# Projection weights by halves of their rows: four raw halves, rings of three split halves in place of two whole blocks

## The chip, the cores and the metric

The kernel runs on one core of one Trainium2 chip. The metric is the device time of one execution in microseconds (us); lower is better. Durations and waits come from one profiled execution, whose engines are named PE (matmul), PEld (PE's weight loads), DVE, ACT, POOL and SP. SP does no arithmetic here: it issues most DMAs, one after the other in a fixed order.

## The reference, cut to what matters

A two-layer encoder trunk over two sequences of 512 and 2048 tokens, T = 2560 tokens in all, width 1024:

```python
p = _rmsnorm(x, norm_w) @ w_in                 # layer 0: 1024 -> 4224 columns
y_a = _rwkv7(r, k, v, w_lat, a_lat, ...)       # a recurrence over tokens, both directions
y_b = _dilated_attention(_rope(q_b), _rope(k_b), v_b)
x = x + concat(y_a * silu(gate_a), y_b * silu(gate_b)) @ w_out
p = _rmsnorm(x, norm_w) @ w_in                 # layer 1: 1024 -> 3088 columns
y = _gla(q, k, v, gate_lat, ...) * silu(gate)  # chunked gated linear attention, both directions
x = x + y @ w_out
```

The change touches the two products with `w_in`, the input projections. All is float32.

## The kernel before, in words

**The projections.** Tokens are taken in five tiles of 512, output columns in blocks of 128: 33 blocks of layer 0 and 25 of layer 1 (one of them 16 columns wide). For a token tile `xprep` (lines 228 to 253) loads and normalises x, transposes it to eight tiles of 128 features by 512 tokens, and splits each into a high part `xh` and a low part `xl` of a reduced float type. `dense` (line 273) then goes through the blocks. The weights of a block are eight slices of 128 rows (k = 0 to 7). Each weight is split in the same way into `wh` and `wl`, and the product is the sum of three: wh·xh + wh·xl + wl·xh. So a block is 24 matmuls of 128x128 by 128x512 on line 287, summed into one bank `pd` of PSUM (two such banks take turns). In most blocks the 16 matmuls with `wh` come first and the 8 with `wl` after them; in the first and last block of a tile's pass the three of each k stand together. There are 5 · 33 + 5 · 25 = 290 blocks in the program; the first 165 of them, of layer 0, are called blocks 0 to 164 here, in the order in which they run.

**How a block's weights come.** `wfetch` (line 255) issues on SP two DMAs of 256 KB (line 258), rows k = 0 to 3 into tile `w0`, rows 4 to 7 into `w1`. Each of the two has one buffer. `wsplit` (line 262) makes `wh` and `wl` for all eight k: of the first half DVE rounds `w` to `wh` (line 266) and subtracts to get `wl` (line 267); of the second half ACT rounds and POOL subtracts. The tiles `wh` and `wl` hold a whole block and have two buffers each. In 4-byte words of a partition that is 2 · 512 raw and 4 · 1024 split, 20 KB.

A raw buffer is free again when its subtraction is done; a buffer of `wh` or `wl` when the last matmul of the block that reads it is done.

**What follows a block.** `even_sink` and `odd_sink` empty the bank: a copy to `st` on ACT (line 307) for the RWKV columns, two products with the rotary tables on DVE (line 317), or a tanh on ACT and a product on DVE (line 341) for the gates.

**What lies beside.** Layer 0: while tile n is projected, `prep` (line 400) makes the recurrence's factors of tile n - 1, with work on all engines and stores of 1 MB (`d_f`, line 480), and `inverts` (line 546) runs long sequences of small DVE operations. Then the recurrence of layer 0 runs beside attention, then the output projection of layer 0 (line 1022), then the projections of layer 1 partly beside the GLA scans, and at the end the output projection of layer 1.

**What sets the order.** Generators are woven by ratio (`mix`) into one program order; a scheduler then lays out every engine's instructions by a simulated time line. The result is one fixed list for each engine (and for each DMA issuer); on the chip each works through its list strictly in order, and an instruction that waits holds back all behind it. `order` rows below are pieces of these lists.

Of the kernel before, what the change touches and what calls it, by code (L numbers as in the profile page):

```python
# [11 lines left out]
F32 = mybir.dt.float32  # L12
F32R = mybir.dt.float32r
# [3 lines left out]
OP = mybir.AluOpType  # L17
# [100 lines left out]
class Trunk:  # L118
# [133 lines left out]
            yield 430  # L252
        xT[:] = tiles

    def wfetch(self, src, m):
        ws = [self.wpool.tile([128, 4, 128], F32, name=f"w{h}", bufs=1) for h in range(2)]
        for h, w in enumerate(ws):
            self.nc.sync.dma_start(w[:, :, :m], src[:, 4 * h:4 * h + 4])
        return ws

    def wsplit(self, ws, m):
        nc = self.nc
        wh, wl = (self.wpool.tile([128, 8, 128], F32R, name=n, bufs=2) for n in ("wh", "wl"))
        for h, (w, e) in enumerate(zip(ws, (nc.vector, nc.gpsimd))):
            k = slice(4 * h, 4 * h + 4)
            (nc.vector.tensor_copy, nc.scalar.copy)[h](wh[:, k, :m], w[:, :, :m])  # L266
            e.tensor_tensor(wl[:, k, :m], w[:, :, :m], wh[:, k, :m].bitcast(F32), op=OP.subtract)  # L267
        return wh, wl

    def dense(self, parts, xT=None):  # L270

        nc = self.nc
        flat = [(p, n, *job) for p, (_, jobs) in enumerate(parts) for n, job in enumerate(jobs)]
        cur = self.wsplit(self.wfetch(*flat[0][2:4]), flat[0][3])
        xT = [] if xT is None else xT
        for i, (p, n, _, m, sink) in enumerate(flat):
            if n == 0 and parts[p][0]:
                yield from parts[p][0](xT)
            wh, wl = cur
            if i + 1 < len(flat):  # L280
                cur = self.wsplit(self.wfetch(*flat[i + 1][2:4]), flat[i + 1][3])
            ps = self.pd.tile([128, 512], F32, name="pd")
            three = [((wh, k, hi), (wh, k, lo), (wl, k, hi)) for k, (hi, lo) in enumerate(xT)]
            byk = n == 0 or n == len(parts[p][1]) - 1
            three = [e for t in three for e in t[:3 if byk else 2]] + [t[2] for t in three if not byk]
            for j, (a, k, x) in enumerate(three):
                nc.tensor.matmul(ps[:m], a[:, k, :m], x, start=j == 0, stop=j == 23)  # L287
                if j % 6 == 5:
                    yield 1280
            sink(ps)  # L290


# [1049 lines left out]
```

## Time and profile before

| | |
|---|---|
| median of 3 runs | 4348.38 us (4346.02 to 4360.76) |
| the profiled execution | 4351.36 us |
| its span, first to last instruction | 4349.3 us |
| mean granted TensorE clock, share of full speed | 0.918 |
| PE busy | 3915.0 us (90%), 28760 matmuls |
| DVE / ACT / POOL busy | 2608.4 (60%) / 1774.4 (41%) / 1481.2 (34%) us |
| DMA moved | 653.67 MB, 150 GB/s |

Busy time of PE counts overlapping matmuls once; since a matmul's end is modelled, a busy PE can still be one at half clock. "A <- B" in a list of waits means that A's engine stood idle until B ended; where an instruction waits for several things, the one that came last is named.

### The profile page before, as it was taken

The numbers are of one execution on the slowest core, as the hardware profiler recorded it, in microseconds if no ns is written. First come the engines' busy times: TensorE is split into PE (matmuls) and PEld (weight loads), VectorE is DVE, ScalarE is ACT, GpSimd is POOL, SyncE is SP. The second block draws the span as 40 slices with busy tenths as digits, with TensorE's granted clock in tenths as the row PEclk, the third lists the DMA queues.
The fourth block names the chain that finished last, engine by engine and source line by source line (L and its number), as shares of the span: only waits on it lengthen the run. The fifth ranks groups of instructions, "written<-read, shape, count | busy, mean of one in ns | idle before, by whom it ended". The sixth has DMA issues, their size and how long they took to land. (4 is left out here: it accounts for less than half of the span.)

```text
span 4349.3 us, 76736 instructions
## 1 busy us (share of the span) xinstructions
PE 3915.0 (90%) x28760; PEld 3050.4 (70%) x28760; DVE 2608.4 (60%) x6092; ACT 1774.4 (41%) x3672; POOL 1481.2 (34%) x1431
## 2 busy tenths in 40 slices
PE   5888789888878898999999997899999999998997
PEld 4666667676656676667776765688777887776776
DVE  3669577686787846545566766323335344567775
ACT  3442434333515234434454544121335344455542
POOL 2454544435545422211122322232333234332331
PEclk9999888989888889778999898999999999999999
DMA  4454444544534545443454443664444444547553
GB/s 146 155 170 150 144 143 160 154 160 147 163 114 138 155 132 150 120 137 108 141 148 131 127 129 103 196 212 138 157 151 153 151 150 133 183 141 233 173 192 125
DMA packets 515503, 653.67 MB, mean 150 GB/s; under 512 B 48188, under 2 KB 340284, under 8 KB 514108
## 3 DMA queue, kind: packets, MB, share of 16 engines
q1 hardware_dynamic: 422044, 560.62, 41.4%
q10 hardware_dynamic: 80464, 72.09, 5.1%
q0 software_dynamic: 12624, 16.06, 1.5%
q8 instruction: 227, 3.72, 0.4%
q14 instruction: 144, 1.18, 0.1%
HBM read 442.48 MB, written 206.36 MB: 149 GB/s over the span
## 5 line engine op out<-in xcount | busy, mean ns | idle before, releaser
L287 PE MATMUL pd<-xh,wh 128*128 128x512 f32 x2320 | 968.9, 420 | 133.3 <-DVE tmp L317 34.7
L287 PE MATMUL pd<-xl,wh 128*128 128x512 f32 (+1 forms) x2320 | 961.4, 415 | 18.9 <-POOL xl L251 18.9
L267 POOL TENSOR_TENSOR wl<-w,wh 128x512 fp32r<-128x512 f32 (+1 forms) x290 | 421.9, 1455 | 936.4 <-ACT wh L266 728.8
L287 PE MATMUL pd<-xh,wl 128*128 128x512 f32 (+1 forms) x2320 | 651.6, 405 | 0.8 <-DVE wl L267 0.8
L287 PEld LDWEIGHTS pd<-xh,wh 128*128 128x128 f32 x2320 | 458.7, 198 | 266.4 <-DVE tmp L317 39.1
L266 ACT CAST wh<-w 128x512 fp32r<-128x512 f32 (+1 forms) x290 | 177.7, 613 | 955.7 <-DMA w<-in_we 533.5
L287 PEld LDWEIGHTS pd<-xl,wh 128*128 128x128 f32 (+1 forms) x2320 | 459.2, 198 | 131.1 <-POOL xl L251 28.0
L287 PEld LDWEIGHTS pd<-xh,wl 128*128 128x128 f32 (+1 forms) x2320 | 442.6, 193 | 100.4 <-issue 4.6
L266 DVE CAST wh<-w 128x512 fp32r<-128x512 f32 (+1 forms) x290 | 148.4, 512 | 461.5 <-DMA w<-in_we 170.0
L267 DVE TENSOR_TENSOR wl<-w,wh 128x512 fp32r<-128x512 f32 (+1 forms) x290 | 247.0, 852 | 110.2 <-PE pd L287 105.0
L1022 PE MATMUL po<-oh,yh 128*128 128x512 f32 x640 | 258.7, 406 | 38.6 <-ACT yh L1011 38.6
L887 ACT ACTIVATE P<-P,O 128x128 f32<-128x128 f32 (+2 forms) x480 | 198.2, 450 | 215.7 <-DVE O L885 209.7
L876 PE MATMUL pS<-Ks,Qs 64*128 64x256 f32 x896 | 270.0, 582 | 6.0 <-DVE O L885 3.2
L1022 PE MATMUL po<-ol,yh 128*128 128x512 f32 x640 | 256.8, 403 | 0.0
L1022 PE MATMUL po<-oh,yl 128*128 128x512 f32 x640 | 251.7, 403 | 2.2 <-DVE yl L1012 2.0
L885 DVE CUSTOM_DVE_ANT_0 P<-pS,msk 128x128 f32<-128x128 f32 (+2 forms) x480 | 153.8, 354 | 144.9 <-PE pS L876 89.0
L925 PE MATMUL pV<-Vt,Pt 128*64 128x65 f32 (+1 forms) x3072 | 184.6, 250 | 32.1 <-DVE O L926 10.2
L925 PEld LDWEIGHTS pV<-Vt,Pt 128*64 128x64 f32 (+1 forms) x3072 | 138.0, 151 | 93.9 <-issue 31.8
L714 POOL TENSOR_TENSOR X<-X,wcs 64x512 f32<-64x512 f32 x76 | 80.3, 1057 | 335.1 <-PE pc L752 171.8
L1009 POOL TENSOR_TENSOR yr<-yr,yg 128x1024 f32<-128x1024 f32 x40 | 97.4, 2435 | 280.9 <-DMA yr<-d_yT 214.1
L876 PEld LDWEIGHTS pS<-Ks,Qs 64*128 64x128 f32 x896 | 148.6, 267 | 52.3 <-issue 13.7
L537 POOL TENSOR_TENSOR PTr<-PTr,wc 128x512 f32<-128x512 f32 x80 | 84.7, 1059 | 258.4 <-PE pg L527 235.7
(280 smaller groups left out, 7709.8 us busy)
## 6 DMA issues: line engine op xcount, KB each, us to landing
w<-in_we SPq DMA_DIRECT2D x330, 256.0 KB
w<-in_wi SPq DMA_DIRECT2D x240, 256.0 KB
d_f<-PT SPq DMA_DIRECT2D x40, 1024.0 KB
PTr<-d_f SPq DMA_DIRECT2D x77, 512.0 KB
d_sg<-st SPq DMA_DIRECT2D x80, 256.0 KB
yr<-d_yT SPq DMA_DIRECT2D x40, 512.0 KB
yg<-d_sg SPq DMA_DIRECT2D x40, 512.0 KB
Vg<-d_gv SPq DMA_DIRECT2D x40, 512.0 KB
```

The lines of the kernel that those rows point to most:

```text
L266: (nc.vector.tensor_copy, nc.scalar.copy)[h](wh[:, k, :m], w[:, :, :m])
L267: e.tensor_tensor(wl[:, k, :m], w[:, :, :m], wh[:, k, :m].bitcast(F32), op=OP.subtract)
L287: nc.tensor.matmul(ps[:m], a[:, k, :m], x, start=j == 0, stop=j == 23)
L537: nc.gpsimd.tensor_tensor(bk, bk, self.wc[:, z, c, :, None].to_broadcast([128, 4, 128]), op=OP.mult)
L714: nc.gpsimd.tensor_tensor(nx, x[lo, 0], self.wcs[:, z, c, :, None].to_broadcast([64, 8, 64]), op=OP.mult)
L876: nc.tensor.matmul(o2, a[o], b[o], start=True, stop=True)
L885: V.tensor_tensor_reduce(P[:, h, :nk], pss[h][:, u, off:off + nk], mask, 1.0, 3e38, op0=OP.add, op1=OP.min, accum_out=m)
L887: nc.scalar.activation(P[:, h, :nk], P[:, h, :nk], AF.Exp, scale=-1.0, bias=m)
L925: nc.tensor.matmul(po[q, h, :], Pt[:r, i, h, q], v[:r, h, :], start=i == 0, stop=i == n - 1)
L1009: nc.gpsimd.tensor_tensor(y, y, g, op=OP.mult)
L1022: nc.tensor.matmul(ps[u][e], a[:, k], b[:, k, c], start=k == 0 and j == 0, stop=k == 7 and j == 2)
```

## The change

The raw tile is now one ring `w` of four halves (512 words each) in place of `w0` and `w1`, and `wh` and `wl` are rings of three halves (512 words each) in place of two whole blocks. In words of a partition: 4 · 512 + 6 · 512, again 20 KB. A generator `weights` walks over the halves of all blocks of a pass: it fetches four halves at the start, and one more after each half that it has split. `dense` keeps two split halves ahead of the one that PE takes up. The engines that split are as before (DVE both steps of a first half, ACT and POOL of a second half). The matmuls of a block are grouped by half: 8 with `wh` and 4 with `wl` of the first half, then the same of the second. Their number, their operands' sizes, the DMAs' number and sizes and the splits' are unchanged.

```diff
-    def wfetch(self, src, m):
-        ws = [self.wpool.tile([128, 4, 128], F32, name=f"w{h}", bufs=1) for h in range(2)]
-        for h, w in enumerate(ws):
-            self.nc.sync.dma_start(w[:, :, :m], src[:, 4 * h:4 * h + 4])
-        return ws
-
-    def wsplit(self, ws, m):
+    def weights(self, flat):
+
         nc = self.nc
-        wh, wl = (self.wpool.tile([128, 8, 128], F32R, name=n, bufs=2) for n in ("wh", "wl"))
-        for h, (w, e) in enumerate(zip(ws, (nc.vector, nc.gpsimd))):
-            k = slice(4 * h, 4 * h + 4)
-            (nc.vector.tensor_copy, nc.scalar.copy)[h](wh[:, k, :m], w[:, :, :m])
-            e.tensor_tensor(wl[:, k, :m], w[:, :, :m], wh[:, k, :m].bitcast(F32), op=OP.subtract)
-        return wh, wl
+        halves = [(src[:, 4 * h:4 * h + 4], m, h) for _, _, src, m, _ in flat for h in range(2)]
+        raw = []
+
+        def fetch():
+            if halves:
+                src, m, h = halves.pop(0)
+                w = self.wpool.tile([128, 4, 128], F32, name="w", bufs=4)
+                nc.sync.dma_start(w[:, :, :m], src)
+                raw.append((w, m, h))
+
+        for _ in range(4):
+            fetch()
+        while raw:
+            w, m, h = raw.pop(0)
+            wh, wl = (self.wpool.tile([128, 4, 128], F32R, name=n, bufs=3) for n in ("wh", "wl"))
+            (nc.vector.tensor_copy, nc.scalar.copy)[h](wh[:, :, :m], w[:, :, :m])
+            (nc.vector, nc.gpsimd)[h].tensor_tensor(wl[:, :, :m], w[:, :, :m], wh[:, :, :m].bitcast(F32), op=OP.subtract)
+            fetch()
+            yield wh, wl
 
     def dense(self, parts, xT=None):
 
         nc = self.nc
         flat = [(p, n, *job) for p, (_, jobs) in enumerate(parts) for n, job in enumerate(jobs)]
-        cur = self.wsplit(self.wfetch(*flat[0][2:4]), flat[0][3])
+        ws = self.weights(flat)
+        split = [next(ws), next(ws)]
         xT = [] if xT is None else xT
-        for i, (p, n, _, m, sink) in enumerate(flat):
+        for p, n, _, m, sink in flat:
             if n == 0 and parts[p][0]:
                 yield from parts[p][0](xT)
-            wh, wl = cur
-            if i + 1 < len(flat):
-                cur = self.wsplit(self.wfetch(*flat[i + 1][2:4]), flat[i + 1][3])
             ps = self.pd.tile([128, 512], F32, name="pd")
-            three = [((wh, k, hi), (wh, k, lo), (wl, k, hi)) for k, (hi, lo) in enumerate(xT)]
             byk = n == 0 or n == len(parts[p][1]) - 1
-            three = [e for t in three for e in t[:3 if byk else 2]] + [t[2] for t in three if not byk]
-            for j, (a, k, x) in enumerate(three):
-                nc.tensor.matmul(ps[:m], a[:, k, :m], x, start=j == 0, stop=j == 23)
-                if j % 6 == 5:
-                    yield 1280
+            for half in range(2):
+                wh, wl = split.pop(0)
+                split.extend(w for w in (next(ws, None),) if w)
+                three = [((wh, k, hi), (wh, k, lo), (wl, k, hi)) for k, (hi, lo) in enumerate(xT[4 * half:4 * half + 4])]
+                three = [e for t in three for e in t[:3 if byk else 2]] + [t[2] for t in three if not byk]
+                for j, (a, k, x) in enumerate(three):
+                    nc.tensor.matmul(ps[:m], a[:, k, :m], x, start=half == 0 and j == 0, stop=half == 1 and j == 11)
+                    if j % 6 == 5:
+                        yield 1280
             sink(ps)
```

How the change moves instructions is seen at two lists, both around block 51 of layer 0, whose second half is the tile `w_4353`. In the changed program all raw halves are called `w` and cannot be told apart by name. Line numbers of the changed kernel stand 9 higher than before from line 287 on; its DMA is line 265, its rounding line 273.

SP's list around the fetches of blocks 50 to 52 (`w_4314` is block 50's second half, `w_4352` and `w_4353` are block 51's, `w_4395` and `w_4396` block 52's). The other rows are loads of `prep` (`p`), its stores (`d_f`, `d_xt`, `d_rkv`) and the rotary table. Before:

```order
L480 DMA d_f_79<-PT 128x8x256
L592 DMA d_xt_94<-XT 128x1024
L379 DMA p<-d_p 128x513
L592 DMA d_xt_94<-XT 128x1024
L258 DMA w_4314<-in_we 128x512
L379 DMA p<-d_p 128x513
L258 DMA w_4352<-in_we 128x512
L491 DMA d_rkv<-tq 2x64x512
L258 DMA w_4353<-in_we 128x512
L379 DMA p<-d_p 128x513
L258 DMA w_4395<-in_we 128x512
L258 DMA w_4396<-in_we 128x512
```

With the change, from the same store of `d_f` to the load of the rotary table:

```order
L489 DMA d_f_79<-PT 128x8x256
L265 DMA w<-in_we 128x512 x3
L388 DMA p<-d_p 128x513
L265 DMA w<-in_we 128x512
L500 DMA d_rkv<-tq 2x64x512
L388 DMA p<-d_p 128x513
L265 DMA w<-in_we 128x512 x5
L356 DMA rope<-in_rope 128x2x512
L265 DMA w<-in_we 128x512 x3
```

The fetches now stand in groups of three and five between the loads and stores of `prep`, where single ones and pairs stood before; no load or store of `prep` left the list.

ACT's list at the same place (`wh<-w` is the rounding of a second half, `r`, `v` and `tq` are `prep`'s, `st<-pd` empties a bank). Before:

```order
L385 ACTIVATE r<-p,c_64 128x512
L266 CAST wh<-w_4314 128x512
L415 ACTIVATE tq<-k,par 128x512
L385 ACTIVATE v<-p,c_64 128x512
L266 CAST wh<-w_4353 128x512
L266 CAST wh<-w_4396 128x512
L327 COPY st<-pd 128x512
L266 CAST wh<-w_4442 128x512
L437 COPY tq<-pp 128x512
```

With the change:

```order
L273 CAST wh<-w 128x512 x2
L394 ACTIVATE r<-p,c_64 128x512
L424 ACTIVATE tq<-k,par 128x512
L394 ACTIVATE v<-p,c_64 128x512
L273 CAST wh<-w 128x512 x4
L446 COPY tq<-pp 128x512
L460 ACTIVATE sg<-pp,hw 128x8x64
L447 DMA d_v<-tq 128x4x128
```

Here two roundings stand ahead of `prep`'s `r`, where before one stood behind it, and four follow each other behind `v`.

## Rows read from the trace of the kernel before

**Rows 1.** Busy time, clock and DMA by stretch of the program

```profile
core 0: us, PE busy (x) PEld busy (x) DVE busy (x) ACT busy (x) POOL busy (x), PEclk, DMA share, GB/s
0.00:1640.00 1640.00, 1350.27 (x9528) 1064.04 (x9529) 1146.90 (x1819) 617.10 (x1168) 733.47 (x713) 0.89 0.47 148
2730.00:3915.00 1185.00, 1169.29 (x5386) 932.19 (x5386) 494.54 (x1010) 447.31 (x812) 379.88 (x333) 0.99 0.50 160
```

**Rows 2.** Chain that ended last, in order of time: start us, us, what

```profile
3021.62 5.46 PE pd L287 x24
3039.36 5.50 PE pd L287 x24
```

**Rows 3.** Waits of PE's weight loads, 0 to 1640 us: us, times, longest

```profile
PEld pd L287 <- DVE tmp L317: 39.1, 11, 7.0
PEld pd L287 <- ACT st L307: 27.0, 15, 4.0
PEld pd L287 <- POOL xl L251: 26.6, 19, 4.3
PEld pd L287 <- DVE st L341: 25.9, 9, 9.5
PEld pd L287 <- ACT wh L266: 19.7, 4, 7.0
PEld pd L287 <- DVE wh L266: 17.1, 4, 8.5
```

**Rows 4.** What ended the idle time before the roundings of line 266, 0 to 1640 us

```profile
  DMA w<-in_we: 703.5, 176
  PE pd L287: 48.2, 20
```

**Rows 5.** Time line around block 51: SP, ACT, POOL, PEld; start us, us, [idle before]

```profile
482.77 0.33 SPq L258 DMA_DIRECT2D w<-in_we  x1
493.97 0.62 ACT L266 CAST wh<-w 128x512 fp32r<-128x512 f32 x1 [12.43 <-DMA w<-in_we]
494.67 1.27 POOL L267 TENSOR_TENSOR wl<-w,wh 128x512 fp32r<-128x512 f32 x1 [10.16 <-ACT wh L266]
494.64 0.29 PEld L287 LDWEIGHTS pd<-xh,wh 128*128 128x128 f32 x1 [7.00 <-ACT wh L266]
```

**Rows 6.** Time line around block 83: SP, DVE, PEld

```profile
773.22 1.19 SPq L258 DMA_DIRECT2D w<-in_we  x1
782.60 0.43 DVE L266 CAST wh<-w 128x512 fp32r<-128x512 f32 x1 [7.26 <-DMA w<-in_we]
783.60 1.28 DVE L317 SCALAR_TENSOR_TENSOR tmp<-pd,rope 128x512 f32<-128x512 f32 x2
784.94 0.29 PEld L287 LDWEIGHTS pd<-xh,wh 128*128 128x128 f32 x1 [6.41 <-DVE tmp L317]
```

**Rows 7.** PEld, first and last of the waits behind a late raw half

```profile
86.98 0.19 PEld L287 LDWEIGHTS pd<-xh,wh 128*128 128x128 f32 x1 [1.45 <-ACT st L307]
...
1481.85 0.19 PEld L287 LDWEIGHTS pd<-xh,wh 128*128 128x128 f32 x1 [2.34 <-ACT wh L266]
```

**Rows 8.** Time line, fetches and roundings of blocks 62 and 63: SP, ACT, POOL

```profile
604.10 1.47 SPq L258 DMA_DIRECT2D w<-in_we  x2
608.58 0.62 ACT L266 CAST wh<-w 128x512 fp32r<-128x512 f32 x1 [1.75 <-DMA w<-in_we]
609.28 1.31 POOL L267 TENSOR_TENSOR wl<-w,wh 128x512 fp32r<-128x512 f32 x1 [4.07 <-ACT wh L266]
614.41 0.62 ACT L266 CAST wh<-w 128x512 fp32r<-128x512 f32 x1 [2.14 <-DMA w<-in_we]
```

**Rows 9.** By stretch, instructions of pd alone: blocks 83 and 65

```profile
784.90:792.50 7.60, 7.56 (x24) 6.08 (x25) 1.28 (x2) 0.00 (x0) 0.72 0.42 114
632.20:637.70 5.50, 5.50 (x26) 4.53 (x26) 0.00 (x0) 0.59 (x1) 1.00 0.37 130
```

**Rows 10.** Who waited for the subtractions of line 267, whole span

```profile
  PEld pd L287: 2.7, 3
  PE pd L287: 0.8, 1
```

**Rows 11.** Waits of PE's weight loads, 2970 to 3915 us

```profile
PEld pd L287 <- DVE st L341: 6.0, 4, 2.3
PEld pd L287 <- DVE wl L267: 1.5, 2, 0.8
```

## The prediction

> **What bounds the kernel now.** I read the busy times by stretch first, to see which engine is full where [rows 1]. From 2730 to 3915 us, where layer 1 is projected, PE is busy 1169.29 of 1185 us at a clock of 0.99; the chain that ended last runs there through the 24 matmuls of block after block, 5.46 to 5.50 us each [rows 2]. Those projections wait for almost nothing [rows 11], so a change of how weights come can't shorten them. From 0 to 1640 us, the projections of layer 0 beside `prep`, PE is busy 1350.27 of 1640 us and its mean clock is 0.89. There is the room, if the change has any.
>
> Next, what PE's weight loads waited for in that stretch [rows 3]: six lines with 155.4 us in 62 waits. Only 36.8 us of them, in eight waits, name a rounding `wh` of line 266. The other names are evictions (`st`, `tmp`: 92.0 us in 35) and the split of x (`xl`: 26.6 us in 19). But an eviction stands in a list behind roundings, so I looked at what the roundings wait for: a raw half that has not landed, 703.5 us in 176 cases, against 48.2 us in 20 for PE [rows 4]. Followed on the time line it looks like this. The second half of block 51 is issued at 482.77, ACT rounds it at 493.97 after 12.43 us of standing still, and PE, which had stood for 7.00 us, goes on at 494.64 [rows 5]. In block 83 the wait is put down to the eviction `tmp`, 6.41 us; yet DVE had stood 7.26 us before the rounding just ahead of it, whose half was issued at 773.22 [rows 6]. I went through all waits of PE for a `pd` matmul in this way: seven eviction waits, 1.45 to 6.41 us, 21.5 us together, hang on a raw half. With the eight that name a rounding that makes 15 waits and 58.3 us; the first and the last of the 15 are in [rows 7].
>
> Why are halves late? Each raw tile has one buffer, so the next fetch is issued only when the subtraction is done. In a calm place that cycle is: issue 604.10, rounding 608.58, subtraction done at 610.59 (609.28 + 1.31), next rounding 614.41 [rows 8]: 5.83 us from rounding to rounding, where PE needs a block every 5.46 us [rows 2]. There is no slack even then, and with a landing of 11 us as in [rows 5] the deficit is some 6 us.
>
> **The change part by part.** One half is 12 matmuls, 5.46 / 2 = 2.73 us.
>
> *Raw halves fetched earlier.* A fetch now follows the subtraction four halves back instead of two: one block, 5.46 us, sooner. SP's list shows fetches in groups, with the loads and stores of `prep` still between them. A weight load's idle time starts while the last matmul still runs, some 0.4 us, so the 15 waits cost PE 58.3 - 15 x 0.4 = 52.3 us. Coming 5.46 us sooner takes away all of each wait up to that length. Three are longer, and keep about 1.1, 0.5 and 2.6 us (their lengths less 0.4 are 6.6, 6.0 and 8.1). Gain: 48 us. What is late next at these places is the eviction itself, without the rounding ahead of it, or DVE's own backlog; bounds: nothing (all 15 replaced) and 52 us.
>
> *The clock.* Block 83, right after its wait, took 7.56 us at a granted clock of 0.72; block 65, after none, 5.50 us at 1.00 [rows 9]. So part of such a block runs at the lower level (1.2 GHz) until PE has worked again. I charge 2.1 us behind each wait of more than 2 us, eleven of the 15, and leave one standing: 10 x 2.1 = 21 us. Bounds: 0 and 15 x 2.1 = 31 us.
>
> *Split rings of three halves.* This part takes something away. Before, a buffer of `wh` was free after the 16 `wh` matmuls of block i - 1 and needed at the start of block i + 1 (first half) or 8 matmuls later (second): 32 and 40 matmuls, 7.3 and 9.1 us, for rounding. Now it is free after 8 of the 12 matmuls of half h - 3 and needed at the start of half h: 28 matmuls, 6.4 us for both. For `wl` of a second half 44 matmuls (10.0 us) become 32 (7.3 us). So an engine that is late by 7 to 10 us now makes PE wait where it did not. The trace has hardly any such wait to price it: PE waited for a subtraction 3.5 us in four cases of the whole span [rows 10]. Lower bound: nothing. Upper bound: 2.7 us at each of the 19 places where POOL's list is late already [rows 3], 51 us. I take three such places, 8 us, near the row that names `wl` itself.
>
> *Everything else costs nothing.* The 24 matmuls of a block, the roundings, subtractions and DMAs are the same in number and size; the grouping by halves only exchanges matmuls of equal length. Roundings stand sooner in ACT's list, ahead of `prep`'s `r`. If one waits there for PE, `prep` waits behind it; before, it waited there for a DMA, and for far longer in sum [rows 4]. The fetches at the start of a pass are four instead of two, beside x's loads, and PE waits for x there in both versions.
>
> Sum: -48 - 21 + 8 = -61 us. Against the profiled execution's 4351.4 us that is 4290; the median of the runs shown lies 3 us lower, so **4287 us**, 1.4% faster. Everything after 1640 us moves forward by as much, since PE's list there is nearly the old one and PE is full in most of it.
>
> **Rivals.**
> 1. *The queues shorten too, faster still.* Rows 3 hold 155.4 - 58.3 = 97 us in 47 waits that I left alone, evictions and `xl` behind busy engines. ACT and DVE no longer stand 703.5 us for raw halves [rows 4], and so reach those instructions sooner. If half of it goes: 4287 - 48 = 4239. Against it: much of that is DVE's own long runs of small operations, which no fetch shortens. Chance 0.15.
> 2. *No change: the landing is not what limits.* PE's waits end mostly with evictions [rows 3]. If these are late for their own engine's sake, or if a half lands late because the DMA queue is full of `prep`'s 1 MB stores (4.5 us from issue to rounding in rows 8, 11.2 in rows 5) and an earlier request only waits longer in the same queue, the waits stay: 4335 to 4361, most likely 4345. Against it: in block 83 DVE stood idle, not busy, ahead of the eviction [rows 6]. Chance 0.13. The Trainium skill has a rule that points this way, on its page "DMA: Bandwidth & Descriptors", section "Anatomy of one DMA" (given there for the GpSimd path): a fixed 2.0 us plus the bytes over 436 GB/s, by which a half of 256 KB would land in an estimated 2.6 us, the old cycle would be about 4.5 us, shorter than a block, and the change would bring nothing. Rows 8 and 5 disagree with it, at 4.5 and 11.2 us from issue to rounding.
> 3. *Slower: the ring of three halves becomes the wait.* Place: the second halves' subtraction on POOL and the first halves' on DVE, between `prep`'s and `xprep`'s work. Price: up to 2.73 us, the lead that is lost, at each block where the engine is late by more than 7.3 us. It decides from 69 / 2.73 = 25 such blocks of the 165 on; at 40 the sum is -69 + 109 = +40, and the time 4388. For it: DVE is busy 1146.90 of the 1640 us [rows 1] and works in bursts. Against it: rows 10. Chance 0.10.
>
> **How the numbers follow.** The forecast has 0.62, with a range of its own of 4262 to 4320: 48 + 31 without any new wait gives 4269, and half the gain with 8 us of new waits 4322. The range for 8 in 10 reaches to rival 1, taken to 52 + 31 + 45 us below 4348, some 4222, and up into rival 2, to 4345; outside are rival 3 and the slower part of rival 2, and a little below. A run can be told from no change at about 0.3%, 13 us. Faster by more than that: the forecast and rival 1, 0.62 + 0.15, less 0.01 for a tail, 0.76; same 0.14; slower 0.10.
>
> **What would show it.** Right: between 0 and 1640 us the waits of line 296's weight loads for a rounding nearly gone and the sum of the six lines near 100 us; the roundings' waits for a DMA far below 703.5 us, and those for PE above 48.2 us; blocks of 5.5 us in a row where 7.5 us stood; a mean clock above 0.89 there; the stretch of layer 1 unchanged. Wrong: PE's waits for evictions as long as before though no rounding waits for a DMA (rival 2), or waits for `wl` on POOL and DVE of tens of us (rival 3).

## The result, and the profile after

The changed kernel takes **4232.31 us** (median of 4 runs, 4229.2 to 4238.83); the kernel before, beside it, 4351.86 (4 runs, 4346.02 to 4360.76). The ratio is 0.9726 [0.9704, 0.9747]: 2.7% faster, some 120 us. The forecast was 4287, a gain of 61: the sign is right and the time lies in the range, but the gain is twice the forecast's, next to rival 1's 4239. The profiled execution took 4229.2 us, its span is 4227.4 and its mean clock 0.931.

First the busy times by stage, with the windows cut at the same work in both kernels: the projections of layer 0 (blocks 0 to 164), the stretch of recurrence, attention and the output projection of layer 0, the projections of layer 1, and the rest. The kernel before, with columns as in [rows 1]:

```profile
0.00:1628.00 1628.00, 1339.58 (x9366) 1055.38 (x9368) 1138.48 (x1791) 610.74 (x1151) 729.04 (x708) 0.89 0.47 149
1628.00:2978.00 1350.00, 1245.73 (x13222) 939.38 (x13222) 751.72 (x2584) 557.43 (x1377) 326.50 (x313) 0.89 0.48 142
2978.00:3913.00 935.00, 927.00 (x4320) 736.64 (x4318) 410.74 (x865) 405.77 (x754) 316.68 (x299) 0.99 0.48 152
3913.00:4349.00 436.00, 402.67 (x1859) 318.97 (x1858) 307.45 (x854) 200.47 (x390) 108.96 (x111) 0.95 0.56 180
```

The changed kernel:

```profile
0.00:1514.00 1514.00, 1294.17 (x9340) 1029.45 (x9340) 1159.48 (x1791) 615.96 (x1149) 720.76 (x707) 0.92 0.51 160
1514.00:2852.00 1338.00, 1236.85 (x13248) 934.44 (x13247) 752.38 (x2585) 556.75 (x1381) 327.05 (x314) 0.90 0.48 143
2852.00:3787.00 935.00, 929.70 (x4353) 739.53 (x4352) 419.62 (x873) 416.23 (x763) 303.07 (x300) 1.00 0.48 152
3787.00:4227.00 440.00, 399.80 (x1824) 315.27 (x1822) 304.01 (x844) 197.49 (x382) 106.17 (x110) 0.94 0.56 178
```

The gain lies where it was forecast: the first stage is 114 us shorter, the others -12, 0 and +4. Within it two things fell. PE's idle time went from 1628 - 1339.58 = 288.4 to 1514 - 1294.17 = 219.8 us, 69 less. And PE is busy 45 us less with the same work (1339.58 to 1294.17; a few matmul records are missing in each), at a clock of 0.92 in place of 0.89. At two levels, full and half, 0.89 means that the lower one held for about 2 · 0.11 · 1628 = 358 us, 0.92 for 2 · 0.08 · 1514 = 242 (each within some 16 us, since the clock is given to two digits).

Next, what stands before the matmuls of a block, by operand (the list of PE's lines in the first stage: count, busy us, mean ns, idle time before them and its releasers). Before:

```profile
L287 PE MATMUL pd<-xh,wh 128*128 128x512 f32 x1320 | 569.1, 435 | 128.2 <-DVE tmp L317 34.7 <-DVE st L341 22.5 <-ACT st L307 21.0
L287 PE MATMUL pd<-xl,wh 128*128 128x512 f32 x1320 | 563.4, 427 | 18.3 <-POOL xl L251 18.3
L287 PE MATMUL pd<-xh,wl 128*128 128x512 f32 x1320 | 373.0, 410 | 0.8 <-DVE wl L267 0.8
```

After:

```profile
L296 PE MATMUL pd<-xh,wh 128*128 128x512 f32 x1320 | 545.7, 416 | 56.3 <-DVE tmp L326 24.4 <-DVE st L350 11.8 <-ACT st L316 7.3
L296 PE MATMUL pd<-xl,wh 128*128 128x512 f32 x1320 | 544.7, 413 | 15.2 <-POOL xl L251 14.9
L296 PE MATMUL pd<-xh,wl 128*128 128x512 f32 x1320 | 397.2, 410 | 4.7 <-DVE wl L274 3.2 <-POOL wl L274 1.4
```

In sum 147.3 us of idle time became 76.2, 71 less, which is as much as PE's whole idle time lost. Other lines of PE changed too, but cancel: the matmuls on `kd`, for one, stood 20 us longer, the transposes of `x` 20 us less. The waits of the weight loads, which answer to [rows 3], first 1525 us:

```profile
PEld pd L296 <- DVE tmp L326: 29.7, 14, 5.2
PEld pd L296 <- POOL xl L251: 20.8, 13, 6.6
PEld pd L296 <- DVE st L350: 15.7, 10, 7.9
PEld pd L296 <- ACT st L316: 11.0, 8, 3.7
PEld pd L296 <- DVE wl L274: 5.1, 4, 2.5
PEld pd L296 <- POOL wl L274: 2.7, 3, 1.4
PEld pd L296 <- ACT wh L273: 1.8, 1, 1.8
```

The six lines of before, 155.4 us, have 79.0 left (29.7 + 20.8 + 15.7 + 11.0 + 1.8, and nothing for DVE's `wh`). For `wl` there are now 7.8 us, where the kernel before had 1.2. Of what the roundings waited for, which answers to [rows 4], the two rows are now:

```profile
  PE pd L296: 218.1, 101
  DMA w<-in_we: 31.2, 8
```

They have changed places: 703.5 us for a raw half became 31.2, and 48.2 us for PE became 218.1. The raw half is there, and the rounding waits for a free buffer. Layer 1 is as it was: its blocks still take 5.46 to 5.50 us [rows 2], by the chain that ended last (first fence), and its weight loads wait little [rows 11] (second fence, 2852 to 3787 us):

```profile
2895.39 5.46 PE pd L296 x24
2901.29 5.50 PE pd L296 x24
```

```profile
PEld pd L296 <- issue: 7.6, 10, 0.8
...
PEld pd L296 <- DVE wl L274: 2.3, 3, 0.8
```

One place of the time line shows both the cure and what is late next. It is the start of block 50, where ACT rounds the second half of block 51; SP, DVE, PEld and ACT, as in [rows 5]:

```profile
456.15 15.75 SPq L265 DMA_DIRECT2D w<-in_we  x5
...
462.41 0.69 DVE L326 SCALAR_TENSOR_TENSOR tmp<-pd,rope 128x512 f32<-128x512 f32 x1 [5.57 <-DMA d_q<-tmp]
...
463.15 0.19 PEld L296 LDWEIGHTS pd<-xh,wh 128*128 128x128 f32 x1 [3.21 <-DVE tmp L326]
...
465.34 0.62 ACT L273 CAST wh<-w 128x512 fp32r<-128x512 f32 x1 [7.90 <-PE pd L296]
```

ACT stood 7.90 us (12.43 in [rows 5]), but for PE's matmuls, which had to free a buffer: here it held PE up by nothing. SP has a group of five fetches under way, ahead of need. What holds PE up is DVE's eviction `tmp`: one of its buffers is still being stored (`d_q`). That wait is new. In the first stage the evictions into `tmp` waited 19.4 us in 8 cases for the store to `d_q` and 6.4 us in 4 for that to `d_k`; before, for no store at all.

### The profile page after: what moved, and what is told of

The parts are those of the page before. It is cut to its first block, busy times and chain, and to the rows that moved or that the text cites. A ratio compares the mean times of both kernels' runs of the same rounds, so it can differ in the third digit from the quotient of the medians.

```text
span 4227.4 us, 76894 instructions
## 1 busy us (share of the span) xinstructions
PE 3860.5 (91%) x28760; PEld 3018.7 (71%) x28760; DVE 2635.5 (62%) x6092; ACT 1786.4 (42%) x3672; POOL 1457.0 (34%) x1431
## 5 line engine op out<-in xcount | busy, mean ns | idle before, releaser
L296 PE MATMUL pd<-xh,wh 128*128 128x512 f32 x2320 | 944.7, 409 | 57.3 <-DVE tmp L326 24.4
L296 PE MATMUL pd<-xl,wh 128*128 128x512 f32 (+1 forms) x2320 | 940.6, 406 | 16.1 <-POOL xl L251 15.8
L296 PE MATMUL pd<-xh,wl 128*128 128x512 f32 (+1 forms) x2320 | 693.2, 405 | 4.7 <-DVE wl L274 3.2
L274 POOL TENSOR_TENSOR wl<-w,wh 128x512 fp32r<-128x512 f32 (+1 forms) x290 | 394.4, 1360 | 664.7 <-PE pd L296 378.4
L296 PEld LDWEIGHTS pd<-xh,wh 128*128 128x128 f32 x2320 | 445.9, 193 | 180.2 <-DVE tmp L326 29.7
L296 PEld LDWEIGHTS pd<-xl,wh 128*128 128x128 f32 (+1 forms) x2320 | 446.6, 193 | 119.9 <-POOL xl L251 22.9
L273 DVE CAST wh<-w 128x512 fp32r<-128x512 f32 (+1 forms) x290 | 160.1, 552 | 354.0 <-PE pd L296 316.7
L274 DVE TENSOR_TENSOR wl<-w,wh 128x512 fp32r<-128x512 f32 (+1 forms) x290 | 231.7, 799 | 68.8 <-PE pd L296 63.4
L894 DVE CUSTOM_DVE_ANT_0 P<-pS,msk 128x128 f32<-128x128 f32 (+2 forms) x480 | 154.0, 354 | 155.4 <-PE pS L885 99.4
```

Of the source, the lines that this page charges most:

```text
L273: (nc.vector.tensor_copy, nc.scalar.copy)[h](wh[:, :, :m], w[:, :, :m])
L274: (nc.vector, nc.gpsimd)[h].tensor_tensor(wl[:, :, :m], w[:, :, :m], wh[:, :, :m].bitcast(F32), op=OP.subtract)
L296: nc.tensor.matmul(ps[:m], a[:, k, :m], x, start=half == 0 and j == 0, stop=half == 1 and j == 11)
L894: V.tensor_tensor_reduce(P[:, h, :nk], pss[h][:, u, off:off + nk], mask, 1.0, 3e38, op0=OP.add, op1=OP.min, accum_out=m)
```

## The experiments

All runs compute the whole result; each was timed in three rounds beside the kernel before, whose median was 4344.44, 4354.37, 4349.61 and 4365.08 us in the four groups below. A ratio is to the kernel before of its own group. That kernel alone differs by up to 21 us between groups, so runs of different groups are compared by their ratios; a difference in medians across groups is a rough one. Profile rows are of the layer-0 projections.

### How many raw halves

`raw2_split3`: two raw halves in the shared ring.

```diff
-                w = self.wpool.tile([128, 4, 128], F32, name="w", bufs=4)
+                w = self.wpool.tile([128, 4, 128], F32, name="w", bufs=2)
...
-        for _ in range(4):
+        for _ in range(2):
```

> The changed kernel with two raw halves in place of four, rings of three split halves kept (2 of 10 buffers less). Theory D (the gain is the depth of raw halves, each fetched a block earlier): the raw cycle of 5.8 us a block is back, so the roundings wait for DMAs again, over 500 us in the first 1640 us, and the time goes back to that of before or above it, since the split rings are also shorter: 4345 to 4390. Theory G (the gain is that buffers are split and freed by halves): most of the gain stays, 4230 to 4270.

`raw3_split3`: the same with three in both places.

> The changed kernel with three raw halves, split rings of three. Theory D: one more half cuts the cycle to 5.8 us per one and a half blocks, under PE's 5.46 us per block in calm places but not where a half takes 8 to 11 us to land: between, 4250 to 4300. Theory G: no change to the changed kernel, 4225 to 4245.

`raw2_split4`: two raw halves and, with `bufs=4` for `wh` and `wl`, four split halves. These are the buffers of the kernel before, held by halves.

> The changed kernel with two raw halves and rings of four split halves: the same number of buffers of each kind as before (2 raw, 8 split), but split, freed and multiplied by halves. Theory D: 4330 to 4360, within 0.5% of before. Theory G: 4230 to 4270. If it lies between, the difference to before is what the halves are worth.

| | median us | ratio |
|---|---|---|
| two raw, four split | 4324.22 | 0.9945 [0.9924, 0.9965] |
| two raw, three split | 4295.83 | 0.9887 [0.9867, 0.9906] |
| three raw, three split | 4218.11 | 0.9707 [0.9691, 0.9723] |
| four raw, three split (the change) | 4232.31 | 0.9726 [0.9704, 0.9747] |

What the roundings waited for, with two raw halves and three split, then with three and three:

```profile
  DMA w<-in_we: 519.9, 132
  PE pd L296: 72.4, 33
```

```profile
  DMA w<-in_we: 243.2, 56
  PE pd L296: 118.8, 60
```

The first stage with two and with three raw halves, both with three split ones:

```profile
0.00:1570.00 1570.00, 1303.63 (x9331) 1026.83 (x9332) 1150.16 (x1791) 610.84 (x1147) 731.55 (x707) 0.92 0.48 154
0.00:1512.00 1512.00, 1282.32 (x9311) 1022.17 (x9312) 1147.15 (x1789) 613.13 (x1147) 727.93 (x707) 0.93 0.50 159
```

The third raw half is the largest single step: 4295.83 to 4218.11, 78 us. By the two traces 58 of them lie in the first stage (37 of PE's idle time, 21 of its busy time); the other 19 come behind it, and no run here explains those. Neither theory had it right: two raw halves came out between the ranges of D and G, three below both. The fourth half brings nothing more; the two intervals overlap. It does cut the roundings' waits further, from 243.2 to 31.2 us, but hardly any of that time was on PE's path. To see this, follow each wait of a `pd` weight load in the first stage back, through what released it and through the lists of the other engines, and count it if a rounding that waited for its raw half lies behind it: 30 waits with 65.6 us for two raw halves, 7 with 9.6 us for three, none for four.

With the buffers of before, kept by halves, 20 us were gained. That the shorter rings of split halves came out 28 us faster was in no expectation, and no run here explains it: 15 us of it lie in the first stage by the two traces (its end at 1570 and 1585 us), 15 behind the last projection, where the code is the same. The scheduler lays the lists of all engines anew for each kernel; whether that is the reason was not tried apart.

### The order of the matmuls alone

`before_byhalf`: the kernel before, with the 24 matmuls of a block grouped by half.

```diff
-            three = [e for t in three for e in t[:3 if byk else 2]] + [t[2] for t in three if not byk]
+            by = lambda q: [e for t in q for e in t[:3 if byk else 2]] + [t[2] for t in q if not byk]
+            three = by(three[:4]) + by(three[4:])
```

> The kernel before with one part of the change alone: the matmuls of a block grouped by half (8 with wh, 4 with wl, twice), buffers and fetches as before. Theory D: nothing to win, 4335 to 4365. Theory R (the regrouping itself lets the first half's wl and the second half's wh be needed at better times): 30 us or more faster, 4320 or less.

4325.05 us, 0.9947 [0.9929, 0.9965]: 19 us faster with no buffer changed, between what the two theories gave, and the same as two raw and four split halves. So the gain of that run is most likely the order's, not that of holding weights by halves. The rows of the waits show what moved:

```profile
PEld pd L288 <- DVE wh L266: 17.1, 6, 5.3
PEld pd L288 <- DVE wl L267: 11.0, 9, 2.8
PEld pd L288 <- ACT wh L266: 5.4, 4, 3.3
```

The second half's `wh` on ACT is needed after 12 matmuls in place of 8, and its waits fell from 19.7 us [rows 3] to 5.4; the first half's `wl` is needed sooner, and its waits rose from 1.2 us to 11.0. In sum these two are worth only some 5 us. The roundings still wait 548.1 us for raw halves (703.5 before). More of the gain is in how long PE is busy, as the first stage shows:

```profile
0.00:1586.00 1586.00, 1310.29 (x9336) 1031.18 (x9338) 1144.67 (x1791) 611.81 (x1149) 733.50 (x707) 0.91 0.47 152
```

Against 1628 us with 1339.58 busy, the stage is 42 us shorter: 29 of busy time, at a clock of 0.91 against 0.89, and 13 of idle time; behind it the trace is 15 us longer. Why the order raises the clock no run shows.

`after_blockorder`: the changed kernel's buffers, with the block's old order (16 with `wh`, then 8 with `wl`). The edit also asks for a block's second new half later, behind its 20th matmul (in the first and last block of a pass behind the 12th).

```diff
-                wh, wl = split.pop(0)
-                split.extend(w for w in (next(ws, None),) if w)
...
+                two.append(split.pop(0))
+            split.extend(w for w in (next(ws, None),) if w)
+            three = [((two[k // 4][0], k % 4, hi), (two[k // 4][0], k % 4, lo), (two[k // 4][1], k % 4, hi)) for k, (hi, lo) in enumerate(xT)]
...
+                if j == (11 if byk else 19):
+                    split.extend(w for w in (next(ws, None),) if w)
```

> The changed kernel with its buffers and fetches, but the matmuls of a block in the old order: 16 with wh, then 8 with wl. In the kernel before, grouping by half alone won 19 us. If that was a later need of the second half's wh (which only matters while halves are late), it is worth nothing with four raw halves: 4225 to 4245. If the grouping helps by itself, the 19 us are lost: 4245 to 4260. More than that would say that rings of three need the grouping, since buffers come free later without it.

4210.32 us, 0.9679 [0.9641, 0.9716]. With four raw halves the order by halves shows no gain (the time is below all three ranges of the expectation); the old order was even 22 us faster in the medians (its four runs, 4203.16 to 4216.28, lie below all four of the change), though the two intervals overlap. Its first stage:

```profile
0.00:1492.00 1492.00, 1275.45 (x9384) 1012.32 (x9386) 1133.59 (x1792) 615.31 (x1153) 719.13 (x708) 0.94 0.50 162
```

PE's idle time is 216.6 us, 3 less than with the change; 19 of the 22 us are busy time, at a clock of 0.94 against 0.92.

### Which half has to come early

Separate rings: one raw buffer for first halves and two for second ones, and the reverse; three in all, as in `raw3_split3`.

```diff
-                w = self.wpool.tile([128, 4, 128], F32, name="w", bufs=4)
+                w = self.wpool.tile([128, 4, 128], F32, name=f"w{h}", bufs=(1, 2)[h])
...
-            fetch()
+            fetch(h)
```

> The changed kernel, rings of three split halves kept, with three raw buffers: one for first halves (DVE splits them), two for second halves (ACT rounds, POOL subtracts). Two raw halves gave 4296, three in one ring 4218. Theory Q (most of the gain comes from ACT and POOL no longer standing behind a late second half; in the kernel before ACT stood 533 us for raw halves, DVE 170): most of the 78 us are won, 4215 to 4245. Theory P (what counts is only the half that PE needs next, first halves as much as second): about half, 4250 to 4280.

> The counterpart: two raw buffers for first halves, one for second halves. Theory Q: little won against two raw halves, 4270 to 4300, ACT still standing some 400 us for second halves in the layer-0 stretch. Theory P: about half, 4250 to 4280.

Two for second halves gave 4286.32 us, 0.9857 [0.9811, 0.9903]; two for first halves 4278.69, 0.9835 [0.9797, 0.9874]. In each PE waits for the kind that has one buffer. With two for second halves it is DVE's rounding, with two for first halves ACT's:

```profile
PEld pd L300 <- DVE wh L277: 18.3, 7, 4.5
```

```profile
PEld pd L300 <- ACT wh L277: 48.2, 22, 6.8
```

By the medians that is 10 and 17 us less than two shared halves, and the intervals overlap with theirs (0.9867 to 0.9906), where the shared ring of three takes off 78. The first lies above both theories' ranges, the second fits Q and P alike, so Q falls: most of the gain is not ACT's and POOL's alone. PE takes the halves in turn, and with either kind left at one buffer most of the gain is missing. The same 768 KB are worth several times more as one ring than bound to a kind.

### Another queue, and the ring of `wl`

`second_from_pool`: the fetches of second halves are issued by POOL instead of SP.

```diff
-                nc.sync.dma_start(w[:, :, :m], src)
+                (nc.sync, nc.gpsimd)[h].dma_start(w[:, :, :m], src)
```

> The changed kernel with the fetches of second halves issued from POOL's queue instead of SP's. SP stood 597 us in the layer-0 stretch waiting for a subtraction before a fetch, with loads and stores of prep behind; POOL needs no wait for its own subtraction, but pays some 0.7 us for an issue (its store d_q took 708 ns). If the remaining waits of layer 0 come from SP's list: 10 to 40 us faster, 4190 to 4222. If not, POOL's 290 issues (200 us of its time) make it slower: 4235 to 4270.

4223.07 us, 0.9711 [0.9664, 0.9757], not told apart from the change, and between what the two theories gave. So it decides little, beyond this: unloading SP's queue wins nothing more that shows.

`blockorder_pool`: the same in the old order.

> The old order of matmuls, four raw halves, second halves fetched from POOL's queue. With the matmuls by half POOL's fetches changed 4232 to 4223. If the two effects add: 4195 to 4208, the fastest so far. If POOL's issues only trade places with SP's: 4205 to 4220.

4223.61 us, 0.972 [0.9687, 0.9752]. The median is 13 us above `after_blockorder` and above both ranges, though the intervals overlap; POOL's queue shows no help in the old order either.

`blockorder_raw3` and `blockorder_raw3_wl4`: the old order with three raw halves, without and with a fourth buffer of `wl`; `raw3_wl4`: three raw halves and that fourth buffer in the order by halves. The edit to the ring:

```diff
-            wh, wl = (self.wpool.tile([128, 4, 128], F32R, name=n, bufs=3) for n in ("wh", "wl"))
+            wh, wl = (self.wpool.tile([128, 4, 128], F32R, name=n, bufs=b) for n, b in (("wh", 3), ("wl", 4)))
```

> The old order of matmuls in the changed kernel (4210) with three raw halves instead of four. With the matmuls by half, three were enough (4218 against 4232). If a shared ring of three covers the landings in either order: 4195 to 4220. If the old order, which needs the second half's wh 4 matmuls sooner, needs the fourth half: 4225 to 4260.

> The same with the buffer that was saved given to wl: a ring of four, wh a ring of three. The prediction charged 8 us for waits on rings of three; in the old order wl of both halves is held to the end of a block, so that its ring should be the tightest. If the ring of wl makes anyone wait who matters: 5 to 20 us faster than the same kernel with three wl. If not: within 8 us of it.

> The matmuls by half, three raw halves, wl a ring of four and wh a ring of three (10 buffers in all, as in the changed kernel). Against raw3_split3 (4218), which differs by the fourth wl alone, this is the price of the ring of three for wl that the prediction put at 8 us. If that price is right or nothing: 4205 to 4222. In the old order of matmuls the fourth wl was worth 32 us; if it is worth as much here: 4180 to 4195.

| | `wl` ring of 3 | `wl` ring of 4 |
|---|---|---|
| old order, three raw | 4239.25, 0.9756 [0.9717, 0.9794] | 4206.95, 0.9682 [0.964, 0.9724] |
| by halves, three raw | 4218.11, 0.9707 [0.9691, 0.9723] | 4217.37, 0.9665 [0.9626, 0.9705] |

In the order by halves the fourth buffer of `wl` is not told apart from none: the medians are the same, the ratios 0.4% apart with intervals that overlap, for the kernel before was slower in the last group. In the old order, where a first half's `wl` is held until the end of the block, the fourth buffer is worth 32 us in the medians (all four runs with it lie below all four without, the intervals just meet), more than the 5 to 20 expected. But a fourth raw half in its place (`after_blockorder`, 4210.32) gives as much, so that it is the ring of `wl` as such isn't shown. With either one the roundings' waits for a raw half fall, from 296.6 us to 182.8 with the fourth `wl` and to 80.9 with the fourth raw half.

The three fastest, `raw3_wl4`, `after_blockorder` and `blockorder_raw3_wl4`, with ratios of 0.9665, 0.9679 and 0.9682, are not told apart. All use no more than the buffers' 20 KB of before.

Four raw halves together with four or more split ones, or two whole raw blocks with the split parts of before, weren't tried.

## Why the prediction was right or wrong

**What bounds the kernel: right.** The first stage gave 114 of the 122 us of span, and the projections of layer 1 none.

**Raw halves fetched earlier: right as a mechanism, and nearly in size.** The 15 waits that I had traced to a raw half, 52.3 us of PE, were forecast to lose 48. Followed back in the same way, no wait of PE in the changed kernel leads to a raw half. `raw2_split3` against `raw3_split3` shows that it is the depth that does it. Rival 2, an earlier request that only waits longer in the queue, falls with the 703.5 us that became 31.2.

**"Everything else costs nothing": wrong, and the step that failed.** I left alone the waits that, by my reading, led to no raw half: of 147.3 us before the `pd` matmuls, 147.3 - 52.3 = 95. After, 76.2 are left, of which 5.9 are for `wl` and ACT's `wh` (3.2, 1.4 and 1.3 in the rows by releaser): 70 stand against 95, 25 us less. That is a quarter of those waits, where rival 1 had a half of them.

Rival 1's mechanism, that engines which no longer stand 703.5 us before roundings come sooner to other work, is not shown by it, for the list of 15 was too short. Four more waits for evictions in the kernel before stand behind a rounding that waited for its half: 2.83 us at 422.46, 2.19 at 552.92, 1.14 at 649.43 and 2.78 at 731.13, in sum 8.9 (some 8 by the halves' lateness, for the rounding at 422.46 had waited only 1.82). The second of them, on ACT, DVE and PEld:

```profile
549.89 0.62 ACT L266 CAST wh<-w 128x512 fp32r<-128x512 f32 x1 [7.98 <-DMA w<-in_we]
551.55 0.60 ACT L340 ACTIVATE tmp<-pd 128x512 f32<-128x512 f32 x1 [0.56 <-issue]
552.18 0.69 DVE L341 SCALAR_TENSOR_TENSOR st<-tmp,pd 128x512 f32<-128x512 f32 x1 [6.06 <-ACT tmp L340]
552.92 0.19 PEld L287 LDWEIGHTS pd<-xh,wh 128*128 128x128 f32 x1 [2.19 <-DVE st L341]
```

Here DVE stood idle for 6.06 us before the eviction: it waited for ACT's tanh, which stands in ACT's list behind the rounding, and that had waited 7.98 us for its half. Counted as in the experiments above, through any length of list, the kernel before has 28 such waits with 85.3 us, against my 15 with 58.3; that is an upper bound. So at least 8 of the 25 us, and at most all of them, belong to the first term, which was then too small; the rest is left to rival 1. The rows fit either: the waits of weight loads for evictions fell from 92.0 us [rows 3] to 56.4 (29.7 + 15.7 + 11.0), 36 less, where I had traced 21.5 to a raw half; those for `xl` fell from 26.6 to 20.8.

The part of that step on the order ("only exchanges matmuls of equal length") was wrong too: alone it was worth 19 us, mostly as less busy time of PE. With four raw halves it shows no gain. The gains overlap, then: 19 for the order alone and 78 for the third raw half are not terms to be added to the others, but two steps of one path (with the shorter rings' 28 between them, and 14 for the fourth half, which is not told apart from nothing, 4344 to 4232).

**The clock: right in sign, half the size, and only in part for the reason given.** I charged 21 us, 2.1 behind each of ten waits. PE's busy time in the first stage fell by 45, and the lower level held about 116 us less (358 to 242, above). The charge went with the 15 waits alone. But with the order alone PE's busy time was already 1310.29 us at a clock of 0.91, and with two raw and three split halves 1303.63 at 0.92, the clock of the changed kernel, while the roundings still waited 519.9 us for raw halves: 29 to 36 of the 45 us came without early halves. Early halves in the old order, on the other hand, bring it to 1275.45. How the 45 us divide, the runs don't show.

**Split rings of three: right.** Charged 8 us from bounds of 0 and 51; the weight loads now wait 5.1 + 2.7 us for `wl` and 1.8 for `wh`, 9.6 together, of which 1.2 for `wl` were there before. [Rows 10] had 3.5 us for the subtractions in the whole span. Rival 3 falls, and `raw3_wl4` shows no clear gain from one more `wl` buffer.

By the first stage's rows, then: -52 for the 15 waits, -25 for the waits left alone, +6 for the rings (all as PE's idle time before `pd`, together 71), -45 of PE's busy time: -116, against the 114 us by which the stage is shorter. The forecast had -48, 0, +8 and -21.

**The rule weighed in rival 2.** Issue to rounding in [rows 8] and [rows 5] was 4.5 and 11.2 us, and the third raw half was worth 78 us. The Trainium skill's "DMA: Bandwidth & Descriptors", section "Anatomy of one DMA", has a fixed 2.0 us plus the bytes over 436 GB/s, an estimate of 2.6 us for such a half, by which two buffers would have sufficed; the measurement decides against it here. The page gives its fit for another issuing path than SP's.

## What to carry to other kernels

When a raw buffer is late, follow every wait of the consumer back, the short ones and those for other work too, before you call the rest unaffected: here the waits left alone lost 25 us beside the 52 that were counted, and at least 8 of these led back to a late half after all. Give a stream of pieces that the consumer takes in turn one shared ring rather than a buffer of each kind. To size it, ask whether the consumer's own waits still lead back to a late piece (65.6, 9.6 and 0 us with two, three and four halves of 256 KB), not what ends the waits of the engines between: with three halves a DMA still ended 243.2 us of the roundings' waits, and a fourth bought nothing that shows. When an order of work seems to gain, try it again after the late transfer is cured.

## What the runs showed that I had not expected

- Two fixed buffers for one kind of half and one for the other gave 4278.69 and 4286.32 us, one ring of three 4218.11: the same memory, 60 to 68 us apart in the medians (0.9835 and 0.9857 against 0.9707).
- Shorter rings of split halves were faster, 4295.83 against 4324.22 us with two raw halves. The cause is open.
- With the weights on time, the rotary evictions on DVE wait for the stores of their own buffers, 25.8 us in 12 cases; before, there was no such wait.
- The mean clock of the first stage rose from 0.89 to 0.92, and to 0.94 in the old order, without any change to the matmuls' number and sizes: 45 us and more of PE's busy time are gone. The order of the matmuls alone took 29 of it, while the roundings still waited 548.1 us for raw halves.
